# Tying one chunk's transposes between two weight steps, and asking for four operand sums one step sooner

## The chip, the cores and the metric

The kernel runs on one core of a Trainium2 chip. TensorE (PE) multiplies, VectorE (DVE) and ScalarE (ACT) do elementwise work, GpSimd (POOL) and SyncE (SP) issue transfers. The metric is the device time of one execution in microseconds (us), the median of several runs. A profiled execution gives, for every instruction, when it started on its engine and how long it took.

## The reference

The program is a two-layer decoder trunk on 512 tokens of width 1024, in float32. Cut to what matters here:

```python
for i in range(DEPTH):                      # DEPTH = 2
    hn = rmsnorm(h, mix_norm_g[i])
    h = h + (sgu_mixer(hn, ...) if i == 0 else retention(hn, positions, ...))
    h = h + swiglu(rmsnorm(h, ffn_norm_g[i]), w_gu[i], w_down[i])
return rmsnorm(h, final_norm_g)

def swiglu(h, w_gu, w_down):
    a, b = split(h @ w_gu, 2)
    return (silu(a) * b) @ w_down

def retention(h, positions, w_in, gn_g, w_out):
    q, k, v, g = split(h @ w_in)            # 4 heads, q and k 256 wide, v and g 512 wide
    q, k = rotary(q), rotary(k)             # rotation by position
    o = decayed causal (q k^T) v            # scores times a decay table, per head
    return (norm(o) * gn_g * silu(g)) @ w_out
```

## The kernel before, in words

**Precision.** A float32 product is made of three matmuls on split operands: every operand is split into a high part (`..h`, a rounded copy made on ACT) and a low part (`..l`, the rest, made on DVE), and `three()` (lines 247 to 249) adds high x high, high x low and low x high. So each weight tile needs one ACT operation (line 216) and one DVE operation (line 223) before TensorE may use it, and activations likewise.

**Tokens to columns.** A layer's input must stand with channels on the partitions. The 512 tokens are four chunks of 128. When a chunk's residual row `X` is final, DVE scales it (`xs`, line 687), TensorE transposes it in 8 pieces (`turn`, line 669, tile `xT`), ACT copies it to `XH` (line 673), DVE makes `XL` (line 674), and two more ACT copies make `xr` (line 706), a plain copy for sums. The chunks come in the order 3, 2, 0, 1; the fourth one to come is chunk 1. The transposes are held in a list, `late`, and called at set points.

**First products.** `project_t` with `halves` multiplies four weight tiles with the tokens 256 to 511 first (chunks 2 and 3); the tokens 0 to 255, which need the fourth chunk, come in a list `rest` (tiles `ps_gl` in the feed-forward layers, `ps_qk` in the retention).

**Seven products.** The large projections (`seven`) use seven products of quarter matrices in place of eight: P1, P7, P6, P2, P5, Q4, P3, in this order here. P1, P2 and Q4 read quarters of the tokens directly; P7, P5, P6 and P3 read sums of quarters, made by `xA` in three steps (sum on DVE, line 737; high part on ACT, line 740; low part on DVE, line 743): P7's sum, P5's sum, P6's made in place from P5's, and P3's made in place from P6's. A sum's steps start when it is asked for, `xparts(p, ask=True)`, and go on by one with each working job. Each product has steps of two weight tiles; with 8 row tiles of weights a unit has two steps per product. P1, P6, P5 and P3 add up in a PSUM tile `X`, P7 and Q4 in `Y`, P2 in `Z`. What an accumulator holds is copied by ACT (`s1` after P1, `y7` after P7, `u2` after P6) before the next product goes on.

**The three places with `between`.** The first unit of each feed-forward layer (`gu0_0`, `gu1_0`) and the first head of the retention (`vg0`) get `rest` as `between`: after P1's first step the fourth chunk is turned (`late_one`), P1's second step follows, and then the `rest` jobs, and after them P7.

**In the first head** the rotation of q and k works on `ps_qk`: four full-width DVE products (`tc`, `ts`, lines 1082 and 1083), then four half-width sums (lines 1086 and 1087), then `q0h`, `k0h` on ACT (line 1090) and `q0l`, `k0l` on DVE (line 1091). The first score matmuls (`sc`) follow P2 in the program.

**What sets the order.** A scheduling pass of the framework puts each engine's instructions into one list before the run, from the order in which the program names them and its own planning; on the chip each engine goes through its list in order and waits at the head of it. `tc.issue_after(ins)` makes what is named inside it stand behind `ins` on that engine's list. PSUM has four slots of tiles, handed out in turn: a new `xT` or accumulator waits until the readers of the slot's former tile are done.

Of the kernel before, what the change touches and what calls it, by code (L numbers as in the profile page):

```python
# [15 lines left out]
P = 128  # L16
# [95 lines left out]
def trunk(ctx, tc, x, positions, mix_g, ffn_g, fin_g, sgu_w_in, sgu_w_s, sgu_b_s, sgu_ln_g, sgu_ln_b,  # L112
          sgu_w_out, ret_w_in, ret_gn_g, ret_w_out, ffn_w_gu, ffn_w_down, invf, decay, out):
    nc = tc.nc
# [50 lines left out]
    ident = const.tile([P, P], F32, name="ident")  # L165
# [85 lines left out]
    xn = {}  # L251
# [69 lines left out]
    def seven(name, w, groups, c1, c2, A, evac, mid=None, look=3, turned=False, order=ORDER, dma=(), onto=(),  # L321
# [103 lines left out]
        def run(i):  # L425
            p, (g, s, nk) = order[i // len(steps)], steps[i % len(steps)]
            if apart and p == "P3" and i % len(steps) == 0:
                acc.update({("W", c): PS(f"W{c}_{name}") for c in range(2)})
            elif p in opens and i % len(steps) == 0:
                acc[chain[p]] = PS(f"{chain[p]}_{name}", (P, 4, H) if turned else (P, 2, T))  # L430
            if s == 0:
                j = asks.index((p, g))
                for q in asks[j:j + (1 if between and i == 0 else look)]:
                    A(*q, ask=True)
            n = i % len(steps)
            if p != order[-1]:
                for c in range(2):
                    matmuls(p, g, s, nk, c)
                if n == len(steps) - 1:
                    evac(p, acc, None)  # L440
                    if p in closes:
                        done(acc[chain[p]])
            elif n < len(steps) - by_chunk:
                for c in range(2):
                    matmuls(p, g, s, nk, c)
            elif n == len(steps) - 1:
                for c in range(2):
                    with tc.issue_after(mm.ins) if apart and c == 1 else nullcontext():
                        for st_ in steps[-by_chunk:]:
                            mm = matmuls(p, *st_, c)  # L450
                    evac(p, acc, c)
                    if apart:
                        done(acc["W", c])
                if not apart:
                    done(acc["X"])
            if mid and (p, n) in mid:
                mid[p, n]()
# [207 lines left out]
    def turn(c, src, name, more=None):  # L665

        ps = PS(f"xT_{name}_{c}", (P, KD, P))
        for k in range(KD):
            nc.tensor.transpose(ps[:, k, :], src[:, k * P:(k + 1) * P], ident)
        if xn.get("name") != name:  # L670
            xn.update(name=name, h=XT(f"XH_{name}"), l=XT(f"XL_{name}"))
        cs = slice(c * P, (c + 1) * P)
        nc.scalar.activation(xn["h"][:, :, cs], ps, AF.Copy)
        nc.vector.tensor_tensor(xn["l"][:, :, cs], ps, f32(xn["h"][:, :, cs]), ALU.subtract)
        if more is not None:
            more(c, ps)
        return ps
# [395 lines left out]
    xparts = xA("r")  # L1073
# [138 lines left out]
    for hd, (first, second, turn_z, values) in enumerate(heads):  # L1212
        rest = ()
        if hd == 0:
            rest = first({("h", 0): lambda: xparts("P7", ask=True), ("h", 1): lambda: xparts("P5", ask=True), ("h", 2): lambda: xparts("P6", ask=True),
                   ("h", 3): lambda: xparts("P3", ask=True)})
        else:
            first({2: heads[hd - 1][2]})
        second({("P6", 1): lambda: outA("P1", 0, ask=True), ("Q4", 0): lambda: outA("P7", 0, ask=True), ("Q4", 1): lambda: outA("P6", 0, ask=True)} if hd == 3 else None, rest)
    t = [list(range(4 * hd, 4 * hd + 4)) for hd in range(HEADS)]  # L1220
    into_x("ro", ret_w_out[0], [(t[0], t[1]), (t[2], t[3])], outA, normed("f1", ffn_g[1:2], raw_copy("f1")),
           {("P1", 1): heads[3][3], ("P7", 1): heads[3][2]})
# [37 lines left out]
```

## Time and profile before

| what | value |
|---|---|
| time, median of 3 runs | 1203.94 us (1203.91 to 1204.99) |
| profiled execution, its own time | 1203.29 us |
| its span, first to last instruction | 1201.5 us |
| PE busy | 1184.5 us, 99% |
| DVE busy | 924.1 us, 77% |
| ACT busy | 643.7 us, 54% |
| POOL busy | 160.8 us, 13% |
| mean granted TensorE clock | 0.998 |

In the rows of a timeline the first number is the start in us from the span's start, the second how long the row took; then engine, line, operation, what is written and read, and a count. In brackets stands how long the engine sat idle before and what released it. Matmuls overlap: the next one starts before the one ahead has ended, so an engine may be late by a part of a matmul without showing idle time; start to start is the surer measure.

### The profile page before, as it was taken

How to read it: one execution, taken by the hardware profiler on the slowest of the kernel's cores; microseconds unless marked ns; L12 is line 12 of the kernel's file. 1: busy time of each engine (PE TensorE's matmuls, PEld its weight loads, DVE VectorE, ACT ScalarE, POOL GpSimd, SP SyncE). 2: the span in 40 equal slices, each digit the busy share in tenths (PEclk: the TensorE clock that was granted, in tenths of full speed). 3: DMA queues.
4: the chain of work that ended last, by engine and by line, in shares of the span. 5: the costliest groups of instructions: out<-in, count | busy, mean ns of one | idle time of the engine just before them, and what ended most of it. 6: DMA issues, size and time to landing. Idle time of an engine off the chain costs nothing.

```text
span 1201.5 us, 18058 instructions
## 1 busy us (share of the span) xinstructions
PE 1184.5 (99%) x7206; PEld 1062.8 (88%) x7206; DVE 924.1 (77%) x1095; ACT 643.7 (54%) x815; POOL 160.8 (13%) x143
## 2 busy tenths in 40 slices
PE   8999999999999999999999999999999999999997
PEld 7888899998999988988888888888899989999986
DVE  5587968698987789787674757879768797666897
ACT  5523755454444547555453645566556554455465
POOL 1000120111110130201101001130121111101210
PEclk9999999999999999999999999999999999999999
DMA  9912968767876788766566457878866788677792
GB/s 314 281 52 54 246 133 206 180 162 216 203 204 145 202 176 266 182 139 172 115 186 145 120 132 170 205 129 282 220 140 173 180 223 221 153 192 191 151 243 99
DMA packets 118980, 216.42 MB, mean 180 GB/s; under 512 B 7496, under 2 KB 20848, under 8 KB 118896
## 3 DMA queue, kind: packets, MB, share of 16 engines
q1 hardware_dynamic: 83888, 148.13, 36.9%
q0 software_dynamic: 34720, 66.61, 33.1%
q8 instruction: 56, 0.92, 0.3%
q10 hardware_dynamic: 288, 0.52, 0.1%
q14 instruction: 28, 0.23, 0.1%
HBM read 212.10 MB, written 2.10 MB: 178 GB/s over the span
## 4 chain that ended last, share of the span: by engine, by line
PE 86%; issue 5%; DMA 4%; DVE 3%; ACT 2%; POOL 1%; SPq 0%; DVEq 0%; POOLq 0%; ACTq 0%
PE X_gu L249 6%; PE X_gu L248 6%; PE X_gu L247 6%; PE Y_gu L248 3%; PE Y_gu L249 3%; PE Y_gu L247 3%; PE X_dn L247 3%; PE X_dn L248 3%; PE X_dn L249 3%; PE X_vg L247 2%; PE X_vg L248 2%; PE X_vg L249 2%; PE ps_qk L247 2%; PE ps_qk L248 2%; PE ps_qk L249 2%
## 5 line engine op out<-in xcount | busy, mean ns | idle before, releaser
L223 DVE TENSOR_TENSOR wl_gu_P<-wr_gu_P,wh_gu_P 128x1024 fp32r<-128x1024 f32 x120 | 144.6, 1220 | 45.1 <-ACT wh_gu_P L216 44.9
L216 ACT ACTIVATE wh_gu_P<-wr_gu_P 128x1024 fp32r<-128x1024 f32 x120 | 122.7, 1052 | 66.2 <-DVE wr_gu_P L375 34.7
L347 POOL DMA_DIRECT2D wr_gu_P<-in_ffn_w_gu x48 | 58.4, 1258 | 381.3 <-DMA wr_gu_P<-in_ffn_w_gu 167.3
L216 ACT ACTIVATE wh_dn_P<-wr_dn_P 128x1024 fp32r<-128x1024 f32 x72 | 69.3, 981 | 51.7 <-DMA wr_dn_P<-in_ffn_w_down 13.3
L223 DVE TENSOR_TENSOR wl_vg_P<-wr_vg_P,wh_vg_P 128x1024 fp32r<-128x1024 f32 x48 | 58.3, 1220 | 34.9 <-ACT wh_vg_P L216 28.7
L223 DVE TENSOR_TENSOR wl_dn_P<-wr_dn_P,wh_dn_P 128x1024 fp32r<-128x1024 f32 x72 | 79.5, 1130 | 3.2 <-issue 2.2
L347 POOL DMA_DIRECT2D wr_vg_P<-in_ret_w_in x26 | 31.5, 1250 | 262.7 <-DMA wr_vg_P<-in_ret_w_in 79.2
L347 POOL DMA_DIRECT2D wr_dn_P<-in_ffn_w_down x36 | 42.0, 1242 | 179.5 <-DMA wr_dn_P<-in_ffn_w_down 92.3
L216 ACT ACTIVATE wh_vg_P<-wr_vg_P 128x1024 fp32r<-128x1024 f32 x48 | 49.6, 1055 | 28.5 <-DMA wr_vg_P<-in_ret_w_in 13.6
L248 PE MATMUL ps_qk<-XL_r,wh_qk 128*128 128x512 f32 (+1 forms) x160 | 55.6, 348 | 0.0
L247 PE MATMUL ps_qk<-XH_r,wh_qk 128*128 128x512 f32 (+1 forms) x160 | 55.3, 348 | 0.0
L249 PE MATMUL ps_qk<-XH_r,wl_qk 128*128 128x512 f32 (+1 forms) x160 | 55.1, 348 | 0.0
L248 PE MATMUL Y_gu<-xP7l_f,wh_gu_P 128*128 128x256 f32 x160 | 45.4, 284 | 0.4 <-DVE xP7l_f L743 0.4
L248 PE MATMUL X_gu<-XL_f,wh_gu_P 128*128 128x256 f32 x160 | 45.4, 283 | 0.0
L249 PE MATMUL X_gu<-XH_f,wl_gu_P 128*128 128x256 f32 x160 | 45.3, 283 | 0.0
L247 PE MATMUL X_gu<-xP6h_f,wh_gu_P 128*128 128x256 f32 x160 | 45.3, 283 | 0.0
L248 PE MATMUL X_gu<-xP6l_f,wh_gu_P 128*128 128x256 f32 x160 | 45.3, 283 | 0.0
L249 PE MATMUL X_gu<-xP6h_f,wl_gu_P 128*128 128x256 f32 x160 | 45.3, 283 | 0.0
L247 PE MATMUL Z_gu<-XH_f,wh_gu_P 128*128 128x256 f32 x160 | 45.3, 283 | 0.0
L248 PE MATMUL Z_gu<-XL_f,wh_gu_P 128*128 128x256 f32 x160 | 45.3, 283 | 0.0
L249 PE MATMUL Z_gu<-XH_f,wl_gu_P 128*128 128x256 f32 x160 | 45.3, 283 | 0.0
L247 PE MATMUL X_gu<-xP5h_f,wh_gu_P 128*128 128x256 f32 x160 | 45.3, 283 | 0.0
(590 smaller groups left out, 4206.8 us busy)
## 6 DMA issues: line engine op xcount, KB each, us to landing
wr_gu_P<-in_ffn_w_gu SPq DMA_DIRECT2D x100, 512.0 KB, 4.8
wr_dn_P<-in_ffn_w_down SPq DMA_DIRECT2D x50, 512.0 KB, 4.9
wr_gu_P<-in_ffn_w_gu POOLq DMA_DIRECT2D x48, 512.0 KB, 7.6
wr_vg_P<-in_ret_w_in SPq DMA_DIRECT2D x40, 512.0 KB, 5.0
wr_dn_P<-in_ffn_w_down POOLq DMA_DIRECT2D x30, 512.0 KB, 7.4
wr_vg_P<-in_ret_w_in POOLq DMA_DIRECT2D x26, 512.0 KB, 7.4
wr_ro_P<-in_ret_w_out SPq DMA_DIRECT2D x20, 512.0 KB, 5.6
wr_qk<-in_ret_w_in SPq DMA_DIRECT2D x32, 256.0 KB, 3.1
```

The lines of the kernel that those rows point to most:

```text
L216: nc.scalar.activation(h, s, AF.Copy)
L223: nc.vector.tensor_tensor(l, s, f32(h), ALU.subtract)
L247: nc.tensor.matmul(o, ah, bh, start=start, stop=False, skip_group_check=True)
L248: nc.tensor.matmul(o, ah, bl, start=False, stop=False, skip_group_check=True)
L249: return nc.tensor.matmul(o, al, bh, start=False, stop=stop, skip_group_check=True)
L347: nc.gpsimd.dma_start(raw[p, 0, g, s][:, 0:nk, :], source(b, g, s, nk), accum_op=ALU.add)
```

## The change

Two edits. In `seven`, when a unit has `between`, the matmuls of the first token half of P1's second step are named inside `issue_after` of the last transpose of the latest chunk (`turn` now keeps it in `xn["turned"]`). And in the retention's first head the four sums are asked for one step sooner: P5's, P6's and P3's after the first, second and third job of `rest`, where they were after the second, third and fourth, and P7's after P1's second step, where it was after the first job of `rest`.

```diff
                 for c in range(2):
-                    matmuls(p, g, s, nk, c)
+                    with tc.issue_after(xn["turned"].ins) if between and i == 1 and c == 0 else nullcontext():
+                        matmuls(p, g, s, nk, c)
...
         for k in range(KD):
-            nc.tensor.transpose(ps[:, k, :], src[:, k * P:(k + 1) * P], ident)
+            xn["turned"] = nc.tensor.transpose(ps[:, k, :], src[:, k * P:(k + 1) * P], ident)
...
         if hd == 0:
-            rest = first({("h", 0): lambda: xparts("P7", ask=True), ("h", 1): lambda: xparts("P5", ask=True), ("h", 2): lambda: xparts("P6", ask=True),
-                   ("h", 3): lambda: xparts("P3", ask=True)})
+            rest = first({("h", 0): lambda: xparts("P5", ask=True), ("h", 1): lambda: xparts("P6", ask=True),
+                   ("h", 2): lambda: xparts("P3", ask=True)})
...
-        second({("P6", 1): lambda: outA("P1", 0, ask=True), ("Q4", 0): lambda: outA("P7", 0, ask=True), ("Q4", 1): lambda: outA("P6", 0, ask=True)} if hd == 3 else None, rest)
+        second({("P6", 1): lambda: outA("P1", 0, ask=True), ("Q4", 0): lambda: outA("P7", 0, ask=True), ("Q4", 1): lambda: outA("P6", 0, ask=True)} if hd == 3 else {("P1", 1): lambda: xparts("P7", ask=True)} if hd == 0 else None, rest)
```

A line is added ahead of most of the program, so a line of 437 or more stands one higher in the changed kernel. The number of instructions is the same. What moves stands in the lists of the engines; names carry a buffer number at their end, and `P2_0_2` is the second weight step of P2.

**First unit of the first feed-forward layer, TensorE.** `X_gu0_0` is P1's accumulator, `xT_f0_1` the fourth chunk's transposes.

```order
 L248 MATMUL X_gu0_0_1532<-XL_f0_1271,wh_gu0_0_P1_0_0_1323 128x256
 L249 MATMUL X_gu0_0_1532<-XH_f0_1270,wl_gu0_0_P1_0_0_1324 128x256
+L670 MATMUL xT_f0_1_1563<-ident_76,xs_f0_1_1385 128x128 x8
 L247 MATMUL X_gu0_0_1532<-XH_f0_1270,wh_gu0_0_P1_0_2_1388 128x256
 L248 MATMUL X_gu0_0_1532<-XL_f0_1271,wh_gu0_0_P1_0_2_1388 128x256
...
 L249 MATMUL X_gu0_0_1532<-XH_f0_1270,wl_gu0_0_P1_0_2_1389 128x256
 L247 MATMUL X_gu0_0_1532<-XH_f0_1270,wh_gu0_0_P1_0_2_1388 128x256
-L669 MATMUL xT_f0_1_1563<-ident_76,xs_f0_1_1385 128x128 x8
 L248 MATMUL X_gu0_0_1532<-XL_f0_1271,wh_gu0_0_P1_0_2_1388 128x256
 L249 MATMUL X_gu0_0_1532<-XH_f0_1270,wl_gu0_0_P1_0_2_1389 128x256
```

The transposes move up by 19 matmuls, to the head of P1's second step. In the second feed-forward layer they move up by two matmuls; in the retention they stood ahead of P1 and still do.

**The same place, ACT, before:**

```order
L706 ACTIVATE xr_f0_0_1_1465<-xT_f0_0_1453 128x4x128
L216 ACTIVATE wh_gu0_0_P6_0_0_1494<-wr_gu0_0_P722_0_0_1246 128x1024
L673 ACTIVATE XH_f0_1270<-xT_f0_1_1563 128x8x128
L216 ACTIVATE wh_gu0_0_P6_0_2_1527<-wr_gu0_0_P722_0_2_1284 128x1024
L216 ACTIVATE wh_gu0_0_P2_0_0_1559<-wr_gu0_0_P221_0_0_1497 128x1024
L1025 ACTIVATE s1_0_0_1600<-X_gu0_0_1532 128x1024
L706 ACTIVATE xr_f0_0_0_1464<-xT_f0_1_1563 128x4x128
L706 ACTIVATE xr_f0_0_1_1465<-xT_f0_1_1563 128x4x128
```

and in the changed kernel:

```order
L707 ACTIVATE xr_f0_0_1_1465<-xT_f0_0_1453 128x4x128
L216 ACTIVATE wh_gu0_0_P6_0_0_1494<-wr_gu0_0_P722_0_0_1246 128x1024
L674 ACTIVATE XH_f0_1270<-xT_f0_1_1563 128x8x128
L216 ACTIVATE wh_gu0_0_P6_0_2_1527<-wr_gu0_0_P722_0_2_1284 128x1024
L707 ACTIVATE xr_f0_0_0_1464<-xT_f0_1_1563 128x4x128
L707 ACTIVATE xr_f0_0_1_1465<-xT_f0_1_1563 128x4x128
L216 ACTIVATE wh_gu0_0_P2_0_0_1559<-wr_gu0_0_P221_0_0_1497 128x1024
L1026 ACTIVATE s1_0_0_1600<-X_gu0_0_1532 128x1024
```

The high part of the fourth chunk, `XH_f0` from `xT_f0_1`, keeps its place behind `wh_gu0_0_P6_0_0`; only the two plain copies `xr` move up, ahead of P2's first weight tile and the copy `s1`.

**First head of the retention, DVE, before:**

```order
L743 SCALAR_TENSOR_TENSOR xP6l_r_5172<-xP5_r_5143,xP6h_r_5171 128x1024
L1082 TENSOR_TENSOR tc_q0_5206<-ps_qk0_0_4897,CS_324 128x1024
L1083 TENSOR_TENSOR ts_q0_5207<-ps_qk0_0_4897,CS_324 128x1024
L1082 TENSOR_TENSOR tc_k0_5212<-ps_qk0_1_4898,CS_324 128x1024
L1083 TENSOR_TENSOR ts_k0_5213<-ps_qk0_1_4898,CS_324 128x1024
L737 TENSOR_TENSOR xP5_r_5143<-xP5_r_5143,xr_r_1_1_4752 128x1024
L1086 TENSOR_TENSOR tc_q0_5206<-tc_q0_5206,ts_q0_5207 128x512
L1087 TENSOR_TENSOR tc_q0_5206<-tc_q0_5206,ts_q0_5207 128x512
L1086 TENSOR_TENSOR tc_k0_5212<-tc_k0_5212,ts_k0_5213 128x512
L1087 TENSOR_TENSOR tc_k0_5212<-tc_k0_5212,ts_k0_5213 128x512
L223 TENSOR_TENSOR wl_vg0_P2_0_2_5085<-wr_vg0_P221_0_2_5048,wh_vg0_P2_0_2_5084 128x1024
L743 SCALAR_TENSOR_TENSOR xP3l_r_5201<-xP5_r_5143,xP3h_r_5200 128x1024
```

and in the changed kernel:

```order
L744 SCALAR_TENSOR_TENSOR xP6l_r_5148<-xP5_r_5119,xP6h_r_5147 128x1024
L738 TENSOR_TENSOR xP5_r_5119<-xP5_r_5119,xr_r_1_1_4752 128x1024
L1083 TENSOR_TENSOR tc_q0_5207<-ps_qk0_0_4897,CS_324 128x1024
L1084 TENSOR_TENSOR ts_q0_5208<-ps_qk0_0_4897,CS_324 128x1024
L1083 TENSOR_TENSOR tc_k0_5213<-ps_qk0_1_4898,CS_324 128x1024
L1084 TENSOR_TENSOR ts_k0_5214<-ps_qk0_1_4898,CS_324 128x1024
L744 SCALAR_TENSOR_TENSOR xP3l_r_5177<-xP5_r_5119,xP3h_r_5176 128x1024
L223 TENSOR_TENSOR wl_vg0_P2_0_2_5089<-wr_vg0_P221_0_2_5048,wh_vg0_P2_0_2_5088 128x1024
L1087 TENSOR_TENSOR tc_q0_5207<-tc_q0_5207,ts_q0_5208 128x512
L1088 TENSOR_TENSOR tc_q0_5207<-tc_q0_5207,ts_q0_5208 128x512
L1087 TENSOR_TENSOR tc_k0_5213<-tc_k0_5213,ts_k0_5214 128x512
L1088 TENSOR_TENSOR tc_k0_5213<-tc_k0_5213,ts_k0_5214 128x512
```

P3's sum (the third operand row on `xP5_r`, from `xr_r_1_1`) moves up ahead of the four full-width rotation products, and P3's low part and `wl_vg0_P2_0_2` move up ahead of the four half-width sums. Ahead of these rows P7's sum moves up past one weight tile, `wl_vg0_P2_0_0`. On ACT the order of this stretch does not change: `xP6h`, `xP3h`, `wh_vg0_P5_0_0`, `q0h`, `y7_0`, `wh_vg0_P5_0_2`, `k0h`, `u2_0`.

**First head of the retention, TensorE at the end of P2, before:**

```order
L248 MATMUL Z_vg0_5297<-wl_vg0_P2_0_2_5085,XH_r_4747 128x512
L249 MATMUL Z_vg0_5297<-wh_vg0_P2_0_2_5084,XL_r_4748 128x512
L247 MATMUL sc0_0_5339<-q0h_5210,k0h_5216 128x512
L247 MATMUL X_vg0_5050<-wh_vg0_P5_0_0_5235,xP5h_r_5141 128x512
L248 MATMUL X_vg0_5050<-wl_vg0_P5_0_0_5236,xP5h_r_5141 128x512
```

and in the changed kernel:

```order
L248 MATMUL Z_vg0_5297<-wl_vg0_P2_0_2_5089,XH_r_4747 128x512
L249 MATMUL Z_vg0_5297<-wh_vg0_P2_0_2_5088,XL_r_4748 128x512
L247 MATMUL sc0_0_5339<-q0h_5211,k0h_5217 128x512
L248 MATMUL sc0_0_5339<-q0l_5212,k0h_5217 128x512
L247 MATMUL X_vg0_5050<-wh_vg0_P5_0_0_5236,xP5h_r_5117 128x512
```

A second score matmul, which reads `q0l`, now stands ahead of P5's first matmul; before, it stood 13 matmuls behind it. Further on, in the rest of this head and the first product of the next one, score matmuls and the matmuls of scores with values (`pv`) take other places among their neighbours.

## The prediction

> **What bounds the kernel now.** I read the page first, then the timeline of TensorE for every place where it waits, and then, at the places that the change touches, the timelines of ACT and DVE.
>
> ```profile
> PE 1184.5 (99%) x7206; PEld 1062.8 (88%) x7206; DVE 924.1 (77%) x1095; ACT 643.7 (54%) x815; POOL 160.8 (13%) x143
> ```
>
> TensorE is busy for 99% of the span. Neither edit adds or removes a matmul, so the change can only move the few waits in front of TensorE. Between the start and the tail there are less than ten of any size, and the touched places hold these, in TensorE's rows (first layer, then retention, then second layer):
>
> ```profile
> 163.57 0.28 PE L247 MATMUL X_gu<-XH_f,wh_gu_P 128*128 128x256 f32 x1
> 168.73 1.04 PE L669 MATMUL xT_f<-ident,xs_f 128*128 128x128 f32 x8
> 169.52 0.36 PE L248 MATMUL X_gu<-XL_f,wh_gu_P 128*128 128x256 f32 x1
> 170.08 0.28 PE L249 MATMUL X_gu<-XH_f,wl_gu_P 128*128 128x256 f32 x1
> 171.36 0.50 PE L247 MATMUL ps_gl<-XH_f,wh_gl 128*128 128x256 f32 x2 [1.01 <-ACT XH_f L673]
> 172.84 0.39 PE L248 MATMUL ps_gl<-XL_f,wh_gl 128*128 128x256 f32 x1 [0.98 <-DVE XL_f L674]
> ...
> 519.17 0.40 PE L248 MATMUL Y_vg<-wl_vg_P,xP7h_r 128*128 128x512 f32 x1
> 520.10 0.50 PE L249 MATMUL Y_vg<-wh_vg_P,xP7l_r 128*128 128x512 f32 x1 [0.52 <-DVE xP7l_r L743]
> 525.22 0.39 PE L247 MATMUL X_vg<-wh_vg_P,xP6h_r 128*128 128x512 f32 x1
> 530.66 0.39 PE L247 MATMUL Z_vg<-wh_vg_P,XH_r 128*128 128x512 f32 x1
> 533.38 0.39 PE L247 MATMUL Z_vg<-wh_vg_P,XH_r 128*128 128x512 f32 x1
> 534.05 0.50 PE L248 MATMUL Z_vg<-wl_vg_P,XH_r 128*128 128x512 f32 x1 [0.28 <-DVE wl_vg_P L223]
> 536.67 0.39 PE L247 MATMUL sc<-q0h,k0h 128*128 128x512 f32 x1
> 537.27 0.50 PE L247 MATMUL X_vg<-wh_vg_P,xP5h_r 128*128 128x512 f32 x1 [0.21 <-ACT u L1143]
> ...
> 881.06 0.40 PE L247 MATMUL ps_gl<-XH_f,wh_gl 128*128 128x256 f32 x2
> ```
>
> What the reader is to see are the brackets, and the distances from start to start, which show a wait even where matmuls overlap. From P1's first matmul (163.57) to the transposes lie 43 matmuls of 256 columns (24 of the first step, 19 of the second), so one takes 5.16 / 43 = 0.12 us. From P6's first matmul (525.22) to P2's (530.66) lie 24 of 512 columns, so one takes 0.227. In the first layer, then, 171.36 comes 1.28 behind a matmul that takes 0.12, so 1.16 are lost, and 172.84 comes 1.48 behind two, so 1.24 are lost: 2.40 us. In the retention 520.10 lost 0.93 - 0.23 = 0.70, 534.05 lost 0.67 - 0.23 = 0.44, and 537.27 lost 0.60 - 0.23 = 0.37. At the same place of the second layer (881.06) no bracket stands.
>
> **First layer: the tie moves the transposes, not what waits.** The eight transposes take 168.73 to 169.52, 0.79 us, wherever they stand. They move up by 19 matmuls of 0.12, so `xT` is ready 2.3 us sooner. Who takes it, on ACT and then DVE:
>
> ```profile
> 164.33 1.08 ACT L706 ACTIVATE xr_f<-xT_f 128x512 f32<-128x512 f32 x2 [1.46 <-DVE XL_f L674]
> 169.34 1.06 ACT L216 ACTIVATE wh_gu_P<-wr_gu_P 128x1024 fp32r<-128x1024 f32 x1 [3.92 <-DMA wr_gu_P<-in_ffn_w_gu]
> 170.30 1.00 ACT L673 ACTIVATE XH_f<-xT_f 128x1024 fp32r<-128x1024 f32 x1
> 170.43 1.23 DVE L223 TENSOR_TENSOR wl_gu_P<-wr_gu_P,wh_gu_P 128x1024 fp32r<-128x1024 f32 x1 [5.00 <-ACT wh_gu_P L216]
> 171.57 1.22 DVE L674 TENSOR_TENSOR XL_f<-xT_f,XH_f 128x1024 fp32r<-128x1024 f32 x1
> ```
>
> ACT stood idle for 3.92 us at the head of its list, for P6's weights, which land at 169.3. `XH_f` stands behind that tile, and in the changed kernel's list still does; on DVE `XL_f` likewise stands behind the same tile's low part. So `XH_f` starts at 170.30 in both, the waits at 171.36 and 172.84 stay, and the term is **0**. Bounds: 0, and -2.40 if both waits went. I take 0, since the row before `XH_f` names a transfer, whose issue the change does not touch. What the tie adds as a wait is hidden: the transposes need the slot that the earlier chunk's `xr` copies free (164.33 + 1.08 = 165.41), and P1's first step ends at 163.57 + 24 x 0.12 = 166.45. If those copies came more than that 1.0 us later, P1's second step, which is now queued behind the transposes, would wait for them, and every microsecond would count. The two `xr` copies that move up on ACT (1.08 together) push P2's first weight tile and the copy `s1` back by that much; they lie beside the 96 matmuls of `ps_gl` (11.5 us) and all of P7, which come first. In the second layer the transposes move by two matmuls, 0.24 us, and nothing on TensorE waited for them: 0.
>
> **Retention: DVE.** The old order, with P7's and P5's sums in the first row:
>
> ```profile
> 516.41 2.35 DVE L737 TENSOR_TENSOR xP_r<-xr_r,xr_r 128x1024 f32<-128x1024 f32 x2
> 518.82 1.22 DVE L743 SCALAR_TENSOR_TENSOR xP7l_r<-xP_r,xP7h_r 128x1024 fp32r<-128x1024 f32 x1
> 523.57 1.23 DVE L743 SCALAR_TENSOR_TENSOR xP6l_r<-xP_r,xP6h_r 128x1024 fp32r<-128x1024 f32 x1 [1.13 <-ACT xP6h_r L740]
> 524.71 1.22 DVE L1082 TENSOR_TENSOR tc_q<-ps_qk,CS 128x1024 f32<-128x1024 f32 x1
> 529.24 1.22 DVE L737 TENSOR_TENSOR xP_r<-xP_r,xr_r 128x1024 f32<-128x1024 f32 x1
> 530.37 0.68 DVE L1086 TENSOR_TENSOR tc_q<-tc_q,ts_q 128x512 f32<-128x512 f32 x1
> 532.78 1.22 DVE L223 TENSOR_TENSOR wl_vg_P<-wr_vg_P,wh_vg_P 128x1024 fp32r<-128x1024 f32 x1
> 533.91 1.22 DVE L743 SCALAR_TENSOR_TENSOR xP3l_r<-xP_r,xP3h_r 128x1024 fp32r<-128x1024 f32 x1
> 536.18 1.22 DVE L1091 TENSOR_TENSOR q0l<-tc_q,q0h 128x1024 fp32r<-128x1024 f32 x1
> ```
>
> A full-width operation takes 1.13 us start to start (532.78 to 533.91, and four from 524.71 to 529.24), a half-width one 0.60 (four from 530.37 to 532.78). P7's sum passes one weight tile, but P5's sum still stands ahead of `xP7l`, so that starts at 518.68 (the weight tile and two sums from 515.27), not 518.82: **-0.14** at 520.10. The rest shrinks to 0.05 by `xP6l` (523.52).
>
> Now the new order. P3's sum follows `xP6l`, which reads the tile that it overwrites, so it starts at 524.8; the four rotation products at 525.9 to 529.3; `xP3l` at 530.5; `wl_vg` of P2's second step at 531.6, done at 532.8. TensorE wants that at 533.38 + 0.23 - 0.14 = 533.47: the wait at 534.05 goes, **-0.44**. The half-width sums follow at 532.74, where they began at 530.37: **2.37 us later**. q's two are done at 532.74 + 0.60 + 0.68 = 534.0, k's two at 532.74 + 3 x 0.60 + 0.68 = 535.2. `q0l` starts at 536.3, where it stood at 536.18, so DVE itself is level again: what stands behind it has the same work ahead of it.
>
> **Retention: ACT, behind those sums.** This list does not change:
>
> ```profile
> 530.54 1.06 ACT L740 ACTIVATE xP3h_r<-xP_r 128x1024 fp32r<-128x1024 f32 x1 [7.01 <-DVE xP_r L737]
> 532.46 1.05 ACT L1090 ACTIVATE q0h<-tc_q 128x1024 fp32r<-128x1024 f32 x1
> 533.41 1.00 ACT L1140 ACTIVATE y<-Y_vg 128x1024 f32<-128x1024 f32 x1
> 534.31 1.05 ACT L216 ACTIVATE wh_vg_P<-wr_vg_P 128x1024 fp32r<-128x1024 f32 x1
> 535.26 1.05 ACT L1090 ACTIVATE k0h<-tc_k 128x1024 fp32r<-128x1024 f32 x1
> 536.21 1.01 ACT L1143 ACTIVATE u<-X_vg 128x1024 f32<-128x1024 f32 x1
> ```
>
> ACT's idle 7 us ahead of `xP3h` end sooner (P3's sum at 524.8), and `xP3h` and the weight tile are out of the way by 528. But `q0h` now waits for q's sums: 534.1 instead of 532.46, **+1.62**. Behind it ACT runs without a gap to `u`, so all shift by the same: `k0h` 536.9 to 537.95, `u` 537.85 to 538.85. Queued there are P5's second weight tile, `k0h` for the scores, and `u`, the copy that frees P5's accumulator.
>
> **Retention: TensorE.** P6 and P2 run 0.14 sooner and without the old wait: P2 starts at 530.52 and ends 24 x 0.227 later, at 535.96. The first score matmul then waits for `k0h`: 538.0, 2.0 us lost. The second one finds `q0l` (536.3 + 1.2) ready: 538.2. P5 waits for `u`: 538.9, where it was 537.27: 1.63 later with one matmul more behind it (0.23). Sum: **+1.40 us**. As a balance: new waits 2.0 + 0.45; old ones gone 0.14 + 0.44 + 0.37 and 0.1 of slack behind 534.05.
>
> From P5 on DVE makes its low parts when it did: the high part of P5's second tile is done at 534.31 + 1.62 + 1.05 = 537.0, and DVE wants it at 537.4. TensorE meets them 1.4 us later than before, so nothing further is late. The moved `pv` and score matmuls take the same time wherever they stand, and I price them at 0: before, no wait stands among them, and the 1.4 us are a new cover. Bounds for the retention: -1.05 if the old waits go and the new ones are covered (0.14 + 0.44 + 0.37 + 0.1), and +2.4 if DVE's whole shift reached TensorE. The chain lies row by row in between, so +1.4.
>
> **Sum.** 0 + 0 + 1.40, on the profiled execution's 1203.29: 1204.7. The median of the runs lies 0.65 above that execution (1203.94), so the forecast for the median is **1205.3 us**, +0.12%. About 0.2%, 2.4 us, is what a measurement of this kernel can tell from no change; so this reads as no change.
>
> **The rivals.** *The tie pays.* If `XH_f` came right behind the transposes, 2.40 us would go in the first layer; with the retention's +1.4 that is -1.0, **1202.9**. For it: that is the largest wait of the middle of the kernel, and the transposes do move. Against: the 3.92 us bracket on ACT. Chance 0.10.
>
> *The retention pays,* its old waits go and no new one comes: -1.05, **1202.9**. For it: P3's sum ends ACT's 7 us of waiting. Against: the two DVE operations now ahead of q's sums. Chance 0.08. Both together: -3.45, **1200.5**, chance 0.05.
>
> *The moves are covered,* the late `k0h` costs what the old waits cost: 0, **1203.9**. For it: 0.95 us of old waits to use up. Against: a shift of 1.62. Chance 0.12.
>
> *Slower: the new wait trips the clock.* At the start of the span TensorE sat idle like this:
>
> ```profile
> 8.20 1.94 PE L669 MATMUL xT_in<-ident,X 128*128 128x128 f32 x8 [2.70 <-DMA X<-in_x]
> ...
> 6.00:9.00 3.00, 0.80 (x4) 0.83 (x5) 2.57 (x3) 1.75 (x3) 0.00 (x0) 0.84 0.95 346
> 9.00:12.00 3.00, 3.00 (x16) 2.79 (x15) 1.89 (x4) 1.04 (x2) 0.00 (x0) 0.59 1.05 375
> 170.00:173.00 3.00, 1.01 (x7) 0.60 (x6) 2.36 (x2) 1.31 (x2) 0.93 (x1) 1.00 1.13 208
> ```
>
> An idle piece of 2.70 us was followed by a granted clock (the column behind the engines) of 0.84 and 0.59, which is 3 x 0.16 + 3 x 0.41 = 1.7 us of full speed lost; two idle pieces with 1.99 us between them in 170 to 173 left it at 1.00. The new wait is one piece of 2.0 and one of 0.45, between the two. If it trips: 1.4 + 1.7 = 3.1, **1207.0**. It decides where the idle piece nears 2.7 us. The Trainium skill, TensorE: Matmul & The Clock Gate, section "What's actually happening", has the clock fall to half after an idle window of about 3.4 us that runs freely; by that rule 2.0 us would not trip it. The row of 2.70 us shows that less in one piece sufficed here, with little work around it. Chance 0.10.
>
> **How the numbers follow.** Forecast 0.55, the rivals 0.45 as given. Forecast, covered and each single gain count as same, except that the forecast lies only 1.0 us below the line of slower: I give 0.06 of its 0.55 to slower. Faster 0.05 + 0.01 of the single gains = 0.06, slower 0.10 + 0.06 = 0.16, same 0.78. The range runs from a single gain, with a little of the runs' spread, to the clock's case: **1202.6 to 1207.2**; the likeliest case alone has 1204.6 to 1206.2.
>
> **What would show it.** In the changed profile: ACT still idle for P6's weights ahead of `XH_f` and TensorE's two waits of about 1 us ahead of `ps_gl`; no wait on `wl_vg` in `Z_vg`; a wait of about 2 us ahead of the first `sc`, released by `k0h`, and one of about 0.4 ahead of P5, by `u`; clock 1.00 there. Wrong would be: `XH_f` ahead of the landing, `sc` without a wait, or a new wait among the `pv` matmuls.

## The result, and the profile after

| | before | changed |
|---|---|---|
| time, median (20 runs each, same chip) | 1205.00 us | 1206.29 us |
| ratio of the runs, with its 95% interval | | 1.0014 (1.0008 to 1.0021) |
| profiled execution, its own time | 1203.29 us | 1205.48 us |
| its span | 1201.5 us | 1203.5 us |
| mean granted TensorE clock | 0.998 | 0.997 |

The kernel became slower by 0.14%, which is 1.7 us of 1205.0 (1.0 to 2.5 by the interval); the medians differ by 1.3. One run of the changed kernel (1965 us, granted clock 0.556) and, in the first four experiments, one of the kernel before (1293 us, 0.849) stand apart from all others, and the ratios leave them out. TensorE's line of the page, after:

```profile
PE 1184.8 (98%) x7206; PEld 1063.1 (88%) x7206; DVE 924.6 (77%) x1095; ACT 643.7 (53%) x815; POOL 160.8 (13%) x143
```

The busy time is what it was, 1184.8 against 1184.5; what came on top is waiting. TensorE's timeline of the changed kernel at the touched places (first feed-forward layer; the last three pieces are P1, P7 and the end of P2 in the retention's first head):

```profile
170.75 0.28 PE L249 MATMUL X_gu<-XH_f,wl_gu_P 128*128 128x256 f32 x1
172.12 0.50 PE L247 MATMUL ps_gl<-XH_f,wh_gl 128*128 128x256 f32 x2 [1.10 <-ACT XH_f L674]
173.61 0.39 PE L248 MATMUL ps_gl<-XL_f,wh_gl 128*128 128x256 f32 x1 [0.98 <-DVE XL_f L675]
...
503.05 0.50 PE L247 MATMUL X_vg<-wh_vg_P,XH_r 128*128 128x512 f32 x1 [0.48 <-ACT xr_r L707]
...
520.13 0.40 PE L248 MATMUL Y_vg<-wl_vg_P,xP7h_r 128*128 128x512 f32 x1
520.50 0.50 PE L249 MATMUL Y_vg<-wh_vg_P,xP7l_r 128*128 128x512 f32 x1
...
533.12 0.39 PE L247 MATMUL Z_vg<-wh_vg_P,XH_r 128*128 128x512 f32 x1
533.35 0.39 PE L248 MATMUL Z_vg<-wl_vg_P,XH_r 128*128 128x512 f32 x1
...
536.29 0.39 PE L249 MATMUL Z_vg<-wh_vg_P,XL_r 128*128 128x512 f32 x1
538.53 0.50 PE L247 MATMUL sc<-q0h,k0h 128*128 128x512 f32 x1 [1.85 <-ACT k0h L1091]
538.87 0.40 PE L248 MATMUL sc<-q0l,k0h 128*128 128x512 f32 x1
539.45 0.50 PE L247 MATMUL X_vg<-wh_vg_P,xP5h_r 128*128 128x512 f32 x1 [0.19 <-ACT u L1144]
```

By the distances from start to start, with 0.12 us for a matmul of 256 columns and 0.23 for one of 512 as in the prediction:

| wait ahead of | before | predicted | changed |
|---|---|---|---|
| `ps_gl`, for `XH_f` | 1.16 | 1.16 | 1.25 |
| `ps_gl`, for `XL_f` | 1.24 | 1.24 | 1.25 |
| `Y_vg`, for `xP7l` | 0.70 | 0.56 | 0.14 |
| `Z_vg`, for `wl_vg` | 0.44 | 0 | 0 |
| `sc`, for `k0h` | 0 | 2.0 | 2.01 |
| P5, for `u` | 0.37 | 0.45 | 0.35 |

Why the first two stand is in ACT's timeline of the changed kernel, and why the fifth came is in its later rows and in DVE's:

```profile
170.10 1.06 ACT L216 ACTIVATE wh_gu_P<-wr_gu_P 128x1024 fp32r<-128x1024 f32 x1 [4.01 <-DMA wr_gu_P<-in_ffn_w_gu]
171.07 1.00 ACT L674 ACTIVATE XH_f<-xT_f 128x1024 fp32r<-128x1024 f32 x1
...
513.59 2.01 ACT L216 ACTIVATE wh_vg_P<-wr_vg_P 128x1024 fp32r<-128x1024 f32 x2 [4.33 <-DMA wr_vg_P<-in_ret_w_in]
...
534.62 1.06 ACT L1091 ACTIVATE q0h<-tc_q 128x1024 fp32r<-128x1024 f32 x1 [5.98 <-DVE tc_q L1088]
537.43 1.05 ACT L1091 ACTIVATE k0h<-tc_k 128x1024 fp32r<-128x1024 f32 x1
538.38 1.02 ACT L1144 ACTIVATE u<-X_vg 128x1024 f32<-128x1024 f32 x1
```

```profile
525.30 1.23 DVE L738 TENSOR_TENSOR xP_r<-xP_r,xr_r 128x1024 f32<-128x1024 f32 x1
...
530.98 1.21 DVE L744 SCALAR_TENSOR_TENSOR xP3l_r<-xP_r,xP3h_r 128x1024 fp32r<-128x1024 f32 x1
532.11 1.21 DVE L223 TENSOR_TENSOR wl_vg_P<-wr_vg_P,wh_vg_P 128x1024 fp32r<-128x1024 f32 x1
533.25 0.68 DVE L1087 TENSOR_TENSOR tc_q<-tc_q,ts_q 128x512 f32<-128x512 f32 x1
```

ACT still stood 4.01 us at the head of its list for P6's weights with `XH_f` behind them. And ACT now stands 5.98 us for q's sums, since on DVE `xP3l` and P2's second low tile pass first.

The retention's four waits sum to 1.51 before and 2.50 after, with one more matmul (0.23) ahead of P5. The two spans differ by 2.0 us; 0.7 of that is there by 170 (170.75 against 170.08), most of it from the wait for the first input chunks at the start of the span (an idle piece of 3.16 us against 2.70), in which the change has no part. Another 0.4 comes at about 453 us, in the first layer's down projection, which neither edit names: TensorE lost 0.86 there before and 1.28 in the changed kernel. So a single pair of profiles can't give the price; the timed runs and the experiments below do.

### The profile page after: what moved, and what is told of

It is laid out like the page before. It is cut to its first block, busy times and chain, and to the rows that moved or that the text cites. A ratio compares the mean times of both kernels' runs of the same rounds, so it can differ in the third digit from the quotient of the medians.

```text
span 1203.5 us, 18054 instructions
## 1 busy us (share of the span) xinstructions
PE 1184.8 (98%) x7206; PEld 1063.1 (88%) x7206; DVE 924.6 (77%) x1095; ACT 643.7 (53%) x815; POOL 160.8 (13%) x143
## 4 chain that ended last, share of the span: by engine, by line
PE 85%; issue 5%; DMA 4%; DVE 4%; ACT 1%; POOL 1%; SPq 0%; DVEq 0%; POOLq 0%; ACTq 0%
PE X_gu L248 6%; PE X_gu L249 6%; PE X_gu L247 6%; PE Y_gu L248 3%; PE Y_gu L249 3%; PE Y_gu L247 3%; PE X_dn L248 3%; PE X_dn L249 3%; PE X_dn L247 3%; PE X_vg L247 2%; PE X_vg L248 2%; PE X_vg L249 2%; DMA wr_gu_P<-in_ffn_w_gu 2%; PE ps_qk L247 2%; PE ps_qk L248 2%
## 5 line engine op out<-in xcount | busy, mean ns | idle before, releaser
L247 PE MATMUL X_gu<-XH_f,wh_gu_P 128*128 128x256 f32 x160 | 45.4, 284 | 0.0
L249 PE MATMUL Y_gu<-XH_f,wl_gu_Q 128*128 128x256 f32 x160 | 45.3, 283 | 0.0
L247 PE MATMUL Y_gu<-XH_f,wh_gu_Q 128*128 128x256 f32 x160 | 45.3, 283 | 0.0
L249 PE MATMUL X_gu<-xP3h_f,wl_gu_P 128*128 128x256 f32 x160 | 45.3, 283 | 0.0
L248 PE MATMUL X_gu<-xP3l_f,wh_gu_P 128*128 128x256 f32 x160 | 45.3, 283 | 0.0
L248 PE MATMUL X_gu<-xP5l_f,wh_gu_P 128*128 128x256 f32 x160 | 45.3, 283 | 0.0
```

Source lines behind the costliest of these rows:

```text
L247: nc.tensor.matmul(o, ah, bh, start=start, stop=False, skip_group_check=True)
L248: nc.tensor.matmul(o, ah, bl, start=False, stop=False, skip_group_check=True)
L249: return nc.tensor.matmul(o, al, bh, start=False, stop=stop, skip_group_check=True)
```

## The experiments

Times are set against the kernel before on the same chip; each ratio is given with its 95% interval.

**The two edits apart.** The tie alone is the changed kernel with this put back:

```diff
-            rest = first({("h", 0): lambda: xparts("P5", ask=True), ("h", 1): lambda: xparts("P6", ask=True),
-                   ("h", 2): lambda: xparts("P3", ask=True)})
+            rest = first({("h", 0): lambda: xparts("P7", ask=True), ("h", 1): lambda: xparts("P5", ask=True), ("h", 2): lambda: xparts("P6", ask=True),
+                   ("h", 3): lambda: xparts("P3", ask=True)})
```

and without the ask for P7 after P1's second step.

> The tie alone, with the four sums asked for where they were. My theory: the transposes come 2.3 us sooner, but XH_f stays behind the weight tile wh_gu of P6 on ACT, which waits for a transfer; so TensorE's waits ahead of ps_gl stay at 1.2 and 1.2 us, and the retention is as before (a wait of about 0.4 us on wl_vg in Z_vg, about 0.4 ahead of P5, none ahead of sc). Time against before: 0 (ratio 1.000, within 0.0007). Rival, the tie pays: -2.4 us, ratio 0.998. Rival, the tie costs what the change lost: +1.3 us, ratio 1.001.

Measured: 1.0001 (0.9992 to 1.0010). TensorE's timeline with the tie alone:

```profile
168.04 1.04 PE L670 MATMUL xT_f<-ident,xs_f 128*128 128x128 f32 x8
172.89 0.50 PE L247 MATMUL ps_gl<-XH_f,wh_gl 128*128 128x256 f32 x2 [0.95 <-ACT XH_f L674]
174.37 0.39 PE L248 MATMUL ps_gl<-XL_f,wh_gl 128*128 128x256 f32 x1 [0.98 <-DVE XL_f L675]
```

The transposes are done 4 us ahead of `ps_gl`, and both waits are there (1.11 and 1.24 lost). The tie is worth nothing here, either way.

The earlier asks alone are the other edit: the kernel before with the asks changed and no tie.

> The four earlier asks alone, without the tie. My theory: all that the change does to the time comes from here: a wait of 2.0 us ahead of the first sc, released by k0h, and 0.35 to 0.45 ahead of P5, by u; the waits on wl_vg in Z_vg and on xP7l in Y_vg are gone. Time against before: +0.8 to +1.4 us, ratio 1.0007 to 1.0012, the same as the whole change within 0.0007. Rival, the loss is the tie's: 0, ratio 1.000. Rival, the old waits cover the new ones: 0, ratio 1.000, with new waits of 1.5 us or less in all.

Measured: 1.0011 (1.0002 to 1.0020), +1.3 us. TensorE's timeline with the asks alone:

```profile
535.34 0.39 PE L249 MATMUL Z_vg<-wh_vg_P,XL_r 128*128 128x512 f32 x1
537.60 0.50 PE L247 MATMUL sc<-q0h,k0h 128*128 128x512 f32 x1 [1.88 <-ACT k0h L1090]
538.52 0.50 PE L247 MATMUL X_vg<-wh_vg_P,xP5h_r 128*128 128x512 f32 x1 [0.18 <-ACT u L1143]
```

The same 2.03 and 0.35 are lost as in the whole change. The four retention waits sum to 2.40 with the asks alone and to 1.01 with the tie alone (0.21, 0.44, 0, 0.36): 1.39 between two kernels in which P6's second weight tile landed at the same distance from P1 (why that matters comes below). So the loss is the asks'.

**Which ask.** The whole change, with P3's sum alone asked for where it was:

```diff
-                   ("h", 2): lambda: xparts("P3", ask=True)})
+                   ("h", 3): lambda: xparts("P3", ask=True)})
```

> The whole change, with one ask put back: P3's sum is asked for after the fourth job again; P7's, P5's and P6's stay a step sooner, and the tie stays. On DVE, P3's sum then stands behind the four full-width rotation products again, and xP3l and P2's second low tile behind the half-width sums. My theory, that the loss comes from these operations standing ahead of q's sums: the 2.0 us wait ahead of sc goes, the wait on wl_vg in Z_vg (0.44) and the one ahead of P5 (0.36) come back. Time against before: 0 (ratio 1.000, within 0.0007), 1.3 us under the change. Rival, that any of the earlier asks costs: 1.0007 to 1.0012, with a wait ahead of sc of 1 us or more.

Measured: 0.9999 (0.9990 to 1.0008). DVE's and TensorE's timelines of this kernel:

```profile
529.89 1.22 DVE L738 TENSOR_TENSOR xP_r<-xP_r,xr_r 128x1024 f32<-128x1024 f32 x1
531.02 0.69 DVE L1087 TENSOR_TENSOR tc_q<-tc_q,ts_q 128x512 f32<-128x512 f32 x1
```

```profile
534.71 0.50 PE L248 MATMUL Z_vg<-wl_vg_P,XH_r 128*128 128x512 f32 x1 [0.39 <-DVE wl_vg_P L223]
537.34 0.39 PE L247 MATMUL sc<-q0h,k0h 128*128 128x512 f32 x1
537.92 0.50 PE L247 MATMUL X_vg<-wh_vg_P,xP5h_r 128*128 128x512 f32 x1 [0.20 <-ACT u L1144]
```

P3's sum is behind the rotation products again, q's sums follow it at once, `sc` has no wait, and the old waits on `wl_vg` and on `u` are back. The four retention waits sum to 1.12, against 2.50 in the change, with the landing of P6's second tile nearly the same in both (10.62 and 10.54 us behind P1's start). One line, the place of one ask, carries the whole loss. The interval reaches up to the lower end of the change's, so the timing alone would be thin; the rows decide.

**What holds `ps_gl`.** The kernel before, with P6's first weight tile of the first feed-forward layer made later and tied behind `XH_f`:

```diff
-                            + [(n - behind.get(p, 0), step) for n, step in prepare(p, *st_)]))
+                            + [(n - (2 if (name, p, st_[1]) == ("gu0_0", "P6", 0) else behind.get(p, 0)), step) for n, step in prepare(p, *st_)]))
...
-                high_()
+                with tc.issue_after(xn["high"].ins) if (name, p, s) == ("gu0_0", "P6", 0) else nullcontext():
+                    high_()
```

(`xn["high"]` is the last `XH` copy.)

> The kernel before, with one thing changed in the first feed-forward layer: the weight tile of P6's first step is made (high part, low part) two jobs later, and its high part is tied behind XH_f of the last chunk. Its transfer is issued as before. So ACT no longer stands at the head of its list for that transfer when the transposes are done. The transposes stay where they were, at 168.7. My theory, that this tile was what held XH_f: XH_f starts at 169.6 instead of 170.3, the wait ahead of ps_gl shrinks from 1.16 to about 0.5, the second stays at about 1.2 (DVE needs 1.2 for XL_f). Time: -0.7 us, ratio 0.9994. Rival, XH_f is held by something else (the transposes' own lateness or the PSUM slot): 0, ratio 1.000. Possible cost: P6's weights come too late for P6 at about 190, which would show as a wait there.

Measured: 0.9984 (0.9975 to 0.9993), -1.9 us. ACT's and TensorE's timelines:

```profile
169.85 1.02 ACT L674 ACTIVATE XH_f<-xT_f 128x1024 fp32r<-128x1024 f32 x1 [4.38 <-PE xT_f L670]
```

```profile
170.93 0.50 PE L247 MATMUL ps_gl<-XH_f,wh_gl 128*128 128x256 f32 x2 [0.53 <-ACT XH_f L674]
172.19 0.39 PE L248 MATMUL ps_gl<-XL_f,wh_gl 128*128 128x256 f32 x1 [0.76 <-DVE XL_f L675]
```

ACT now waits for the transposes and no longer for a transfer, and the two waits shrink to 0.69 and 1.02: 0.69 us less in all, as expected. The runs gained 1.2 us more than that (0.1 to 2.3 by the interval). The profile has one other place of that size, in the first layer's down projection. Before:

```profile
453.19 0.49 PE L247 MATMUL X_dn<-wh_dn_P,h_P5h 128*128 128x512 f32 x1 [0.45 <-ACT wh_dn_P L216]
```

TensorE lost 0.86 there before and nothing in this kernel, where the weight tile that it waits for landed at 449.80 instead of 451.12; with the 0.69 that makes up the 1.5 us between the two profiled spans. The other kernels have 0.7 to 1.3 there, the next one too, which moves the same tile of P6. So it isn't shown that the edit did this, and the rest of the gain stays open.

The same with the change's tie:

> The same, together with the change's tie (and without its earlier asks). My theory: with the weight tile out of the way the tie is worth what it was meant for: the transposes are done at 167.2, XH_f runs at 167.4 to 168.4, XL_f to 169.6, before TensorE asks for them at 170.1; both waits ahead of ps_gl (1.16 and 1.24) go. Time against before: -2.4 us, ratio 0.9980. Rival, what holds ps_gl is not ACT's queue: 0 to -0.7 us, ratio 0.9994 to 1.000.

Measured: 0.9988 (0.9979 to 0.9997), -1.4 us, at the edge of what was expected. TensorE's timeline, then ACT's:

```profile
166.58 1.04 PE L671 MATMUL xT_f<-ident,xs_f 128*128 128x128 f32 x8
170.32 0.40 PE L247 MATMUL ps_gl<-XH_f,wh_gl 128*128 128x256 f32 x2
181.84 0.28 PE L247 MATMUL Y_gu<-xP7h_f,wh_gu_P 128*128 128x256 f32 x1
183.38 0.39 PE L248 MATMUL Y_gu<-xP7l_f,wh_gu_P 128*128 128x256 f32 x1 [1.26 <-DVE xP7l_f L745]
```

```profile
167.65 1.02 ACT L675 ACTIVATE XH_f<-xT_f 128x1024 fp32r<-128x1024 f32 x1 [2.10 <-PE xT_f L671]
175.33 2.96 ACT L216 ACTIVATE wh_gu_P<-wr_gu_P 128x1024 fp32r<-128x1024 f32 x3 [4.28 <-DMA wr_gu_P<-in_ffn_w_gu]
```

Both `ps_gl` waits are gone, so the tie does what its name says once ACT's list allows it. But 1.42 us come back 12 us later, ahead of P7: its operand `xP7` is queued behind P6's second weight tile, whose transfer lands at 175.3 in this kernel as in the one before. TensorE being 2.4 us sooner only meets the next wait for the same transfers.

**A version that beats both.** The tie without the earlier asks, and in the first unit of the first feed-forward layer P7's operand made in one go after P1's second step, with P6's high and low parts behind it:

```diff
+            if (name, p) == ("gu0_0", "P6"):
+                high_later.append(high)
+                low_later.append(low)
+                return [(SUM, total)] if p not in dma else []
             return ([] if p in dma else [(SUM, total)]) + [(HIGH, high), (PREP, low)]
...
+        def p7_then_p6():
+            xparts("P7")
+            for step in (*high_later, *low_later):
+                step()
...
-        unit(0, {("P1", 1): lambda: xparts("P7", ask=True)}, between=rest)
+        unit(0, {("P1", 1): p7_then_p6 if l == 0 else lambda: xparts("P7", ask=True)}, between=rest)
```

> The tie, without the earlier asks of the retention, and in the first feed-forward layer P7's operand is made in one go after P1's second step (sum, high part, low part) and the high and low parts of both weight tiles of P6 only behind it. So ACT and DVE no longer stand at the transfers of P6's weights with XH_f, XL_f and P7's operand queued behind. In the run with the tile moved behind XH_f the two waits ahead of ps_gl (2.4 us) went, but 1.42 came back as a wait for xP7l, since P7's operand stayed behind P6's second tile, which lands at 175.3. My theory: with xP7l ready by about 174 that wait goes too, and the full 2.4 us are kept: ratio 0.9980. Rival, the time is given back further on (P6's weights too late at 187.6, or DVE behind): a new wait in P6 or P2 of the first unit, ratio 0.999 to 1.000.

Measured: 0.9971 (0.9960 to 0.9983), 1200.98 against 1204.39 us. DVE's row of P7's low part, 7 us before TensorE wants it:

```profile
173.59 1.23 DVE L750 SCALAR_TENSOR_TENSOR xP7l_f<-xP_f,xP7h_f 128x1024 fp32r<-128x1024 f32 x1 [1.12 <-ACT xP7h_f L747]
```

Between 160 and 200 us TensorE's timeline of this kernel has no bracket left. The full 2.4 us are kept. The runs gained 3.4 us (2.0 to 4.8 by the interval); what lies above 2.4 isn't explained.

The same order at all three places with `between` (in the second feed-forward layer and in the retention's first head too, with `p7_then_p6` called after P1's second step there):

> The tie and the same order (P7's operand in one go after P1's second step, then the high and low parts of P6's weights) at all three places with rest jobs between P1 and P7: both feed-forward layers and the retention's first head. The retention's other sums are asked for where they were. My theory, that at each place DVE and ACT stand at P6's transfers with P7's operand queued behind: in the retention DVE does two operations of 1.13 us more in its idle time ahead of P6's second tile, so the wait for xP7l in Y_vg (0.15 to 0.7, by when that tile lands) goes, and the sums behind it come about 1 us sooner, so most of the waits on wl_vg in Z_vg (0.44) and on u ahead of P5 (0.36) go too; in the second layer the wait for xP7l in Y_gu (0.2 to 0.6) goes. That is 1.0 to 1.9 us on top of the 2.4 of the first layer: -3.4 to -4.3 us, ratio 0.9964 to 0.9972. Rival, the retention and the second layer have other late operands: 2.4 us as in the first layer alone, ratio 0.9980, with waits of the same size elsewhere.

Measured: 0.9956 (0.9942 to 0.9969), 1199.36 against 1204.43 us, the fastest kernel here, 5 us under the kernel before, where at most 4.3 were expected. For the retention half of the theory is borne out. P7's wait is gone there and in the second layer, but the other sums did not reach TensorE sooner. ACT's and TensorE's timelines:

```profile
512.51 2.01 ACT L216 ACTIVATE wh_vg_P<-wr_vg_P 128x1024 fp32r<-128x1024 f32 x2 [3.11 <-DMA wr_vg_P<-in_ret_w_in]
```

```profile
500.61 0.50 PE L247 MATMUL X_vg<-wh_vg_P,XH_r 128*128 128x512 f32 x1 [0.47 <-ACT xr_r L719]
532.31 0.50 PE L248 MATMUL Z_vg<-wl_vg_P,XH_r 128*128 128x512 f32 x1 [0.81 <-DVE wl_vg_P L223]
```

In this profile P6's second tile landed 11.90 us after P1's start, later than in any other (10.53 in the version before it), and DVE's chain behind it reaches TensorE at the wait on `wl_vg`, 0.96 lost there. The chain itself is shorter, as expected: P5's sum starts 3.37 us behind the landing, and 4.50 behind it in the kernel before. The later landing took that gain; whether the new order has a part in the landing isn't shown. The retention's waits sum to 1.32 here against 1.11 in the version before it (0.28, 0.46, 0, 0.37). So the profile shows a gain at the second layer's P7 (0.51 lost in the kernel before, 0.24 in the first version, none here) and none over the first version in the retention. That is about 3 us in all, and the rest of the 5 us stays open; that the second version is faster than the first is likely from the ratios, but their intervals overlap.

**The clock.** The last rival had the new wait trip the granted clock. The changed kernel's stretches around the wait (the third number from the end is the clock):

```profile
536.00:539.00 3.00, 1.15 (x6) 0.52 (x4) 3.00 (x3) 3.00 (x4) 0.00 (x0) 1.00 0.60 196
539.00:542.00 3.00, 2.81 (x13) 2.14 (x12) 3.00 (x4) 3.00 (x4) 0.00 (x0) 1.00 0.53 169
```

It did not. How near it was, four kernels show that make the wait longer. Two put operations that leave their tile as it is ahead of q's sums on DVE (one half-width, or three full-width):

```diff
         def rest():
+            if name == "q0":
+                nc.vector.tensor_tensor(ts_[:, 0, :], ts_[:, 0, :], ts_[:, 0, :], ALU.max)
```

> The whole change, with one more half-width operation on DVE ahead of the half-width sums of q (the maximum of a tile with itself, which leaves it as it is); the list then also puts k's sums ahead of q's second. So q0h comes 1.8 us later than in the change, and the idle piece ahead of sc grows from 1.85 to about 3.7 us. My theory, that only the wait itself is paid: 1.3 + 1.8 = +3.1 us against before, ratio 1.0026, and a granted clock of 1.00 in the 3 us behind the wait. Rival, the clock trips once a piece reaches 2.7 us, as at the start of the span: at least 1.7 us more, +4.8 us, ratio 1.004, and a granted clock well under 1.00 behind the wait.

> The same with three full-width operations there (each leaves its tile as it is). The list puts k's sums and one accumulation of Z ahead of q's sums, so q0h comes 5.8 us later than in the change and the idle piece ahead of sc is about 7.6 us. My theory: 1.3 + 5.8 = +7.1 us, ratio 1.0059, if the clock holds; I hold this open here, since the piece is nearly three times the 2.70 us after which the clock was at 0.84 and 0.59 at the start. Rival, the clock trips: 1.7 us or more on top, +8.8 us, ratio 1.0073, and a granted clock under 1.00 in the stretch behind the wait.

and two repeat `k0h`'s copy on ACT, once whole, or once whole and once by half:

```diff
+        def high():
+            if name == "k0":
+                nc.scalar.activation(h, tc_, AF.Copy)
+            nc.scalar.activation(h, tc_, AF.Copy)
```

> The whole change, with k0h's copy on ACT made twice (the same values). k0h and u come about 0.95 us later (one copy, start to start 0.95), so the idle piece ahead of sc grows from 1.85 to about 2.8 us, just past the 2.70 us of the start of the span; the second score matmul pair now also stands ahead of P5, so u's own wait is covered. With the piece at 3.70 us the clock went to half for 3.2 us and 1.6 us were lost; with 1.85 it held. Theory A, that the length of the idle piece decides and the limit lies at or under 2.7: the clock falls to half behind the wait, +1.3 + 0.9 + 1.6 = +3.8 us against before, ratio 1.0031. Theory B, that the start is a case of its own (little work around it) and here it takes more: the clock holds, +2.2 us, ratio 1.0018.

> The same with one half-width copy more (k0h and u about 1.5 us later than in the change), so the idle piece is about 3.3 us. Theory A (limit at or under 2.7): the clock falls, +1.3 + 1.4 + 1.6 = +4.3 us, ratio 1.0036. Theory B (limit above 3.3 here): +2.7 us, ratio 1.0022, and the clock holds at 1.00.

The stretches behind the wait with the copy made twice, and with the half-width operation:

```profile
539.00:542.00 3.00, 1.04 (x5) 0.64 (x5) 3.00 (x4) 2.97 (x4) 0.00 (x0) 1.00 0.43 131
542.00:545.00 3.00, 3.00 (x10) 2.37 (x9) 2.94 (x3) 3.00 (x4) 0.00 (x0) 0.55 0.45 154
545.00:548.00 3.00, 3.00 (x13) 2.37 (x13) 1.30 (x2) 1.55 (x2) 0.00 (x0) 0.88 0.55 178
```

```profile
542.00:545.00 3.00, 3.00 (x8) 2.32 (x9) 2.96 (x3) 3.00 (x4) 0.00 (x0) 0.53 0.55 178
545.00:548.00 3.00, 3.00 (x14) 2.45 (x13) 1.37 (x2) 1.63 (x2) 0.00 (x0) 0.90 0.53 168
```

| kernel | idle piece | clock behind it | full speed lost | ratio (interval) | us |
|---|---|---|---|---|---|
| the change | 1.85 | 1.00 | 0 | 1.0014 (1.0008 to 1.0021) | +1.7 |
| copy made twice | 2.94 | 0.55, 0.88 | 1.7 | 1.0027 (1.0014 to 1.0041) | +3.3 |
| copy 2.5 times | 3.61 | 0.81, 0.62 | 1.7 | 1.0048 (1.0034 to 1.0061) | +5.8 |
| half-width operation | 3.70 | 0.53, 0.90 | 1.7 | 1.0035 (1.0022 to 1.0047) | +4.2 |
| three operations | 7.73 | 0.50, 0.61 | 1.7 | 1.0072 (1.0059 to 1.0086) | +8.7 |

(Lost: each stretch of 3 us by what its clock lacks of 1.00, 3 x 0.45 + 3 x 0.12 = 1.7 in the second row; in the last row from the wait's end at 544.02 on.) In all four the clock fell, 2.94 us of idling included, and the price is the same 1.7 us each time. So the expectation for the half-width operation, that only the wait itself is paid, was wrong. The timed ratios alone would not settle it: only with the copy made 2.5 times is the interval clear of what was expected without a fall (1.0022), and in the other three it reaches that value (1.0018, 1.0026, 1.0059). The clock column settles it for the profiled executions; whether every execution of the copy-twice kernel falls is not shown (its six times reach from 1205.2 to 1209.4).

## Why the prediction was right, and where it was off

*The forecast* was 1205.3 us, +0.12%, read as no change, with 1202.6 to 1207.2. Measured: 1206.29, ratio 1.0014. Part of the distance is the base: the forecast stood on a median of 1203.94 over three runs, and over twenty the kernel before has 1205.0; from there the forecast's 1.4 us lead to 1206.4. The prediction also took 0.2% for the least that a measurement of this kernel can tell from no change. Twenty runs of each tell less: the interval is 0.07% to either side, so 0.14% is clear of zero.

*First layer: the tie moves the transposes, not what waits.* Right, and shown by both sides: with the tie alone the waits stay, with the weight tile out of the way and the tie they go. The chance of 0.10 for "the tie pays" went to a case that the list of ACT rules out.

*But the bound of -2.40 was mis-sized.* The prediction gave 2.40 us for both waits gone and looked no further down. The run that removed them kept about 1.0 by its profile (2.40 - 1.42), since P7's operand stood behind the same transfers. The rival should have stood at 1202.9 + 1.4 = 1204.3. The list of waits at the touched places also left out P7's in the second layer, 0.51 at 893.21 before; with 0.56 in the change it moves nothing in the sum.

*Retention, DVE and ACT.* The order of events was as written: `xP3l` and `wl_vg` ahead of q's sums, `q0h` later, and all of ACT's chain to `u` with it. From the landing of P6's second tile to `q0h` lie 534.62 - 513.59 = 21.03 us after and 532.46 - 513.04 = 19.42 before: 1.61 later, where 1.62 was written.

*Retention, TensorE.* New waits 2.01 and 0.35 (2.0 and 0.45 written), the one on `wl_vg` gone. The sum of 1.40 compares with 1.39 between the two single edits and +1.3 us by the runs of the asks alone.

*The term that was off is P7's old wait.* The step took 0.70 as the kernel's and moved it by 0.14. It isn't the kernel's: it is set by when P6's second weight tile lands, counted from P1's first matmul, and that differs from execution to execution: the change and its four lengthened versions have the same lists of ACT and DVE up to the landing and lie between 10.53 and 11.45. The two rows in the kernel before:

```profile
501.86 0.50 PE L247 MATMUL X_vg<-wh_vg_P,XH_r 128*128 128x512 f32 x1 [0.47 <-ACT xr_r L706]
513.04 2.01 ACT L216 ACTIVATE wh_vg_P<-wr_vg_P 128x1024 fp32r<-128x1024 f32 x2 [4.93 <-DMA wr_vg_P<-in_ret_w_in]
```

From the same two rows (513.59 and 503.05 in the change) of every profile in which P7's sum stands behind that tile:

| P7's sum as in the change | landing after P1's start | wait for `xP7l` |
|---|---|---|
| asks alone | 10.43 | 0.02 |
| half-width operation | 10.53 | 0.15 |
| the change | 10.54 | 0.14 |
| P3's ask put back | 10.62 | 0.22 |
| three operations | 10.89 | 0.50 |
| copy made twice | 10.98 | 0.54 |
| copy 2.5 times | 11.45 | 1.05 |
| **P7's sum as before** | | |
| weight tile behind `XH_f`, with the tie | 10.45 | 0.15 |
| tie alone | 10.46 | 0.21 |
| first version that beats both | 10.53 | 0.28 |
| weight tile behind `XH_f`, no tie | 11.18 | 0.68 |
| before | 11.18 | 0.70 |

In the upper part the wait is the landing less 10.41, within 0.03. At a landing of 10.5 the new place of the sum is worth 0.13 (0.28 against 0.15), which is the -0.14 of the prediction; at 11.18 it would be worth nothing. So the profile of before showed a late landing, and the forecast took a draw for a term.

*The clock* held, as the forecast had it. The point from which it decides, "where the idle piece nears 2.7 us", fits: 1.85 held, 2.94 fell, and the price of 1.7 us was right.

## What to carry to other kernels

Before a producer is moved up, read what its consumer's engine stands at: an engine that goes through its list in order holds everything behind the one tile whose transfer is late, and only moving that tile back lets the earlier producer pay. When that wait is removed, follow the same transfer to the next thing queued behind it, since most of the gain may be given back there. And an ask that is moved "a step sooner" on a busy engine moves other work back; count what it passes on the way to the copies that free accumulators.

## What the runs showed of the hardware that was not expected

The granted clock can fall after the wait is over, and it stays down for a fixed time. Stretches of half a microsecond, with `k0h`'s copy made twice:

```profile
542.00:542.50 0.50, 0.50 (x4) 0.44 (x3) 0.50 (x1) 0.50 (x1) 0.00 (x0) 0.81 0.98 332
...
545.50:546.00 0.50, 0.50 (x3) 0.39 (x2) 0.50 (x1) 0.50 (x2) 0.00 (x0) 0.78 0.00 0
```

Between these two the clock is 0.50. A mean of 0.81 is 0.31 us at full and 0.19 at half, so it fell at 542.31; a mean of 0.78 puts its return at 545.72: 3.41 us at half, or 1.7 lost, and the wait had ended at 540.96 already. Worked out the same way, it fell at 542.18 with the half-width operation (wait over at 541.04), at 540.87 with the copy 2.5 times (540.52), at 540.49 with three operations (in the middle of the wait) and at 8.06 at the start of the span before; the slow piece was 3.41 us long each time (the expectation for the copy made twice took 3.2), and twice that with three operations.

The Trainium skill, TensorE: Matmul & The Clock Gate, section "What's actually happening", has a window of 3413 ns that runs freely: an idle one brings half speed, a busy one full speed again. The length of 3.41 us and the changing distance from the wait agree with that. That the window must be idle throughout does not: with the copy made twice TensorE's idle piece was 2.94 us, less than the window, and in the 3.41 us ahead of the fall at 542.31 TensorE was idle for 2.06 (from 538.90 to 540.96), and at 1.00 it worked for the rest. Since the window runs freely, a piece of idle time can be cut in two by it; 1.85 us in one piece did not reach the limit in the one profile of the change.

The landing of one transfer of 512 KB, counted from the matmul that starts ahead of it, lay between 10.43 and 11.90 us in the thirteen profiles, and with the sum in the change's place it moves TensorE's wait one for one. What sets it was not tried.
